# PEER expert layers: all tiles of the first table plain, a later use of 16 tokens' activations, eight tiles of the second table loaded early

## The chip, the cores and the metric

The kernel runs on one core of a Trainium2 chip. The core has TensorE (matmul; PE, with its weight loads PEld), VectorE (DVE), ScalarE (ACT), GpSimd (POOL) and SyncE (SP, which here issues DMAs), all working side by side on their own queues in program order, and 16 DMA engines. The metric is the device time of one execution in microseconds (us). The median of 3 runs of the kernel before is 1668.15 us (1666.73 to 1670.56).

## What is computed

A decoder trunk of two layers over 256 positions with 1024 features. Layer 0 is multi-head latent attention, layer 1 is native sparse attention; behind each stands a PEER feed-forward layer, and every sub-layer ends in a LayerNorm of `alpha * x + f(x)`. The change lies in the PEER layers, which run twice:

```python
def chunk(xc):
    q = (xc @ w_q).reshape(PEER_CHUNK, PEER_HEADS, 2, PEER_DK // 2)
    sc = jnp.einsum("thpd,hpnd->thpn", q, subkeys)
    s_half, i_half = lax.top_k(sc, PEER_TOPK)
    ...
    best, pos = lax.top_k(cand, PEER_TOPK)
    experts = jnp.take_along_axis(cand_idx, pos, axis=-1)
    g = jax.nn.softmax(best, axis=-1)
    u_e = u[experts]
    v_e = v[experts]
    a = jax.nn.gelu(jnp.einsum("thkd,td->thk", u_e, xc), approximate=False)
    return jnp.einsum("thk,thkd->td", (g * a), v_e)
```

So each token picks 8 x 16 = 128 of 16,384 experts, takes the gelu of its dot product with each picked row of table u, weighs it with the softmax `g`, and sums the picked rows of table v with these weights.

## The kernel before, in words

**Stages.** A PEER layer goes through three stages: projections and routing (`p_wq`, scores, top-k), then **u** (128 tiles of table u, each 128 experts x 1024 features), then **v** (128 tiles of table v). For 192 of the 256 tokens the kernel computes every expert: a u tile gives the dot products of 128 experts with these tokens on TensorE, their gelu goes into a store `A`, and the weight of an expert that a token did not pick is zero. Each of the last 64 tokens (`GT`) has its picked rows gathered from both tables by POOL instead; VectorE takes the dot products (`g_dot`, L554) in u and the weighted sums (`g_mac`, L582) in v. Of the 192 tokens, 176 (`NU`) get their u activations from the u tiles; the other 16 (`GX`) get theirs from gathered rows too, sent through a small DRAM buffer (`xdot` to `xD` to `xact`) and turned on TensorE in `x_weights` (L564).

**Plain and split tiles.** A tile of u is used in one of two ways, which `natural(j)` (L48) decides by the tile's number j. A *plain* tile (`nat`) is loaded straight into one of five places and multiplied in f32 with `xF`, the 176 tokens. A *split* tile goes through the weights' ring: it is loaded into one of four places of `raw4` (`raw`), ScalarE rounds it to `hi` (L157), VectorE takes the rest `lo` (L171), and TensorE multiplies `hi` with both halves of the activations side by side (352 columns) and `lo` with the high half (176 columns); ScalarE copies the second 176 columns out (`half`, L867) and VectorE adds them (L868). Tiles 0 to 43 and 122 to 127 are plain, of 44 to 111 three in four, of 112 to 121 one in three: 104 plain and 24 split ones per layer. The tiles of v are all split, and are loaded two at a time.

**Weights of the experts.** VectorE builds one-hots (`hot`, L731 and L736, for the last four groups L742) for four tokens at a time in `g_gen`. TensorE multiplies them in `g_flush` (`acc<-hot`), two groups at a time, at the beginning of a u tile when two are ready; VectorE and ScalarE put the product into `A` (L765, L767). The gelu of a tile comes one tile later in `u_fin` (L856), and its product with the weights (L859) a tile after that.

**What sets the order.** The program is written out in order by hand; each engine works down its own queue. Per u tile: the flush, the tile's matmuls, `u_fin` of the tile before, a portion of the one-hots by a budget (`run_side`), and about three row dot products in four tiles. `self.defer(n, f)` runs `f` n tiles later. Loads go out on SP in program order: `_snat` issues a plain tile five tiles ahead (`LEADN`), `_sdma` the ring's tiles as far as `_ahead` allows, never beyond `vlim`. `more_raw` opens four further places (`spare`), which lie where the activations `hT` lay; before, it is called at tile 121 of u. `end` closes each u tile and issues what `held` allows.

Of the kernel before, what the change touches and what calls it, by code (L numbers as in the profile page):

```python
# [24 lines left out]
P = 128  # L25
# [14 lines left out]
NROW = 6  # L40
RING, LEAD = 6, 1
LEADN = 5
LATE, LASTS = 112, 122
GB = 0.8
GS = 2.0 ** 15


def natural(j):  # L48
    return j < FIRST or j >= LASTS or (j % 4 != 3 if j < LATE else j % 3 == 0)


class Kern:
# [5 lines left out]
    def plan(self):  # L58
        I, L = self.I, []
        self.v0s, self.spare, self.pairs = [], None, {}  # L60
        self.nh, self.odd, self.nat, self.natural = 0, {}, set(), {}
        if "mla" in self.parts:
            L += [I["a_w_in"][k] for k in range(KC)]
            L += [I["a_wk"][i] for i in range(2)]
            L += [I["a_wq"][i] for i in range(3)]
            L += [I["a_wv"][i] for i in range(2)]
            L += [I["a_wq"][i] for i in range(3, 6)]
            L += [I["a_wo"][i] for i in range(KC)]
        for l in (0, 1):
            if l == 1 and "nsa" in self.parts:  # L70
                L += [I["s_wv"][i] for i in range(4)]
                L += [I["s_wT"][i] for i in range(4)]
                L += [I["b_wg"]]
                L += [I["s_wT"][i] for i in range(4, 8)]
                L += [I["b_wq"][i] for i in range(4)]
                L += [I["b_wq"][i] for i in range(4, 8)]
                L += [I["b_wo"][i] for i in range(KC)] + [I["b_wo"][i] for i in range(KC // 2)]
            if f"peer{l}" in self.parts:
                L += [I["p_wq"][l, i] for i in range(16)]
                self.nat.update(len(L) + j for j in range(P) if natural(j))  # L80
                self.odd.update((len(L) + j, 0) for j in range(P))
                L += [I["p_u"][l, (P - FIRST + j) % P] for j in range(P)]
                self.v0s.append(len(L))
                o = (len(L) - len(self.nat) - self.v0s[0] + sum(i < self.v0s[0] for i in self.nat)) % 4
                self.odd.update((len(L) + j, 1) for j in range(P))
                self.pairs.update((len(L) + j, I["p_v"][l, j:j + 2].rearrange("j i d -> i j d")) for j in range(o % 2, P - 1, 2))
                L += [I["p_v"][l, j] for j in range(P)]
        self.stream = L
        self.v0 = self.vb = self.v0s[0]
        self.rank = [0]  # L90
        for i in range(len(L) + 1):
            self.rank.append(self.rank[-1] + (i not in self.nat))
        self.si = 0
        self.used = 0
        self.sd = 0
        self.sn = 0
        self.slow, self.held, self.vlim = False, 0, 1 << 20
        self.sh = 0
        self.sl = 0
        self.raws, self.his, self.los = {}, {}, {}  # L100
        self.share = False
        self.alt = {}
        self.later, self.now = [], 0
# [101 lines left out]
    def end(self):  # L205

        self.used = self.si - 1
        self._snat()
        self.vlim += 2
        self._sdma(self.held)  # L210
        self.held = self._ahead()

# [286 lines left out]
    def peer(self, l):  # L499
        tc, nc, I = self.tc, self.nc, self.I  # L500
        self.v0 = self.v0s.pop(0)
        with ExitStack() as es:
            pool = lambda st, name: st.enter_context(tc.tile_pool(name=name, bufs=1, reuse_waits="tile"))

# [46 lines left out]
            def g_dot(k):  # L551
                a, c = order[k]
                t, x, d = grow.pop((a, c)), *((gacc, gdot) if a == "n" else (xrow, xdot))
                nc.vector.scalar_tensor_tensor(t, t, 1.0, x, op0=OP.mult, op1=OP.mult, accum_out=d[:, c:c + 1])  # L554
                if (a, c) == ("x", GX - 1):
                    g_row()
                    nc.scalar.activation(xdot, xdot, AF.Gelu)
                    self.defer(1, lambda: nc.gpsimd.dma_start(xD[1].rearrange("s t c -> (s t) c"), xdot))
                    self.defer(3, lambda: nc.gpsimd.dma_start(xact.rearrange("t (s c) -> t s c", s=P // GX),
                                                              xD[1].rearrange("s t c -> t s c")))  # L560
                    self.defer(6, x_weights)
                g_row()

            def x_weights():  # L564
# [268 lines left out]
            pu = None  # L833

            def u_step(j):
                hi, lo = self.nxt()
                ps = self.ps()
                if lo is None:
                    for k in range(KC):
                        self.mm(ps[:, 0:NU], hi[:, k * P:(k + 1) * P], xF[:, k, :], k == 0, k == KC - 1)  # L840
                else:

                    def high(k):
                        self.mm(ps[:, 0:2 * NU], hi[:, k * P:(k + 1) * P], self.hTT[:, k, :, 0:NU], k == 0, k == KC - 1)

                    for k in range(KC - 1):
                        high(k)
                    for k in range(KC):
                        self.mm(ps[:, 0:NU], lo[:, k * P:(k + 1) * P], xhi[:, k, 0:NU], False, False)
                    high(KC - 1)  # L850
                self.end()
                return j, ps, lo is not None

            due = deque()

            def u_fin(x):  # L856
                while due:
                    y, ps = due.popleft()
                    nc.vector.tensor_tensor(y, y, ps, op=OP.mult)  # L859
                if x is None:  # L860
                    return
                j, ps, wide = x
                jj = (P - FIRST + j) % P
                y, n = slot(jj), min(done["g"], NU)
                if wide:
                    t = gat.tile([P, NU], F32, tag="half", name="half", bufs=2)
                    nc.scalar.copy(t, ps[:, NU:2 * NU])  # L867
                    nc.vector.tensor_tensor(ps[:, 0:NU], ps[:, 0:NU], t, op=OP.add)  # L868
                if n:
                    nc.scalar.activation(ps[:, 0:n], ps[:, 0:n], AF.Gelu)  # L870
                    due.append((y[:, 0:n], ps[:, 0:n]))
                if n < NU:
                    nc.scalar.activation(y[:, n:NU], ps[:, n:NU], AF.Gelu)  # L873
                done["a"] = j + 1
# [22 lines left out]
                w_lo(1)  # L897

            dc, dj = 0, None
            self.slow, self.held = True, 0  # L900
            for j in range(P):
                if j == 5:
                    g_x()
                g_flush(2)
                x = u_step(j)
                if j == LASTS - 1:
                    self.slow, self.vlim = False, self.v0 + 1
                    self.more_raw()
                u_fin(pu)
                pu = x  # L910
                run_side(GB if len(A) > 1 else 2.2 if dj is None or j < dj else 1.4)
# [877 lines left out]
```

## Time and profile before

| What | Value |
|---|---|
| median of 3 runs | 1668.15 us |
| the profiled execution | 1670.8 us |
| its span, first to last instruction | 1669.0 us |
| mean granted TensorE clock | 0.993 |
| u of layer 0 and of layer 1, on TensorE | 168.65 to 513.46 us, 1024.86 to 1366.26 us |
| v of layer 0, on TensorE | from 513.46 to about 803 us |
| loads of u tiles | 208 plain, 48 split, 512 KB each |
| loads of v tiles | 127 pairs of 1024 KB, 2 single |
| HBM over the span | 295 GB/s |

The profile is one execution on the chip. A busy share is an average over stages with different limits, so the stages are read by windows. Matmuls are pipelined and their ends are modelled: the time of one is read from the start of one to the start of the next. In a row of a timeline stand the start, the time from the first start to the last end, engine, line, operation, tiles (out<-in) and count, and in brackets how long the engine was idle before it and what released it. A plain f32 matmul of the program stands as two instructions in the profile, so a plain tile has 16.

### The profile page before, as it was taken

The page shows a single profiled execution, that of the slowest core. Times are in us where ns is not written, and L with a number is a line of the kernel's source. Part 1 is how long each engine was busy: PE and PEld are TensorE (multiplying, and loading weights), DVE is VectorE, ACT ScalarE, POOL GpSimd, SP SyncE. Part 2 cuts the span into 40 slices and gives each one's busy share as a digit, 9 for nine tenths or more (in the row PEclk, how much of TensorE's full clock was granted, in tenths as well). Part 3 has the DMA queues.
Part 4 walks back from the last instruction along what each step waited for, and adds up shares of the span by engine and source line. Part 5 has one row for each costly group of instructions (what it writes and reads, how often), then busy time and mean ns, then how long its engine had stood idle before and what let it go on. Part 6 is the DMA issues. An engine that isn't in the chain of part 4 may idle for free.

```text
span 1669.0 us, 28191 instructions
## 1 busy us (share of the span) xinstructions
PE 1605.8 (96%) x9988; PEld 1441.3 (86%) x9988; DVE 1438.9 (86%) x3437; ACT 777.4 (47%) x1675; POOL 524.6 (31%) x426
## 2 busy tenths in 40 slices
PE   7999999999989999999997999999999999999997
PEld 6879999899988888888885789999999898888886
DVE  6788698799987999999778789688899969999998
ACT  6655212333345555556466853123333345555554
POOL 2011133333334444441342211334333325444430
PEclk9999999999999999999999999999999999999999
DMA  7528899899978999998583258999999889999992
GB/s 243 189 84 262 295 362 368 307 342 341 335 274 337 387 359 349 356 356 311 172 257 95 70 193 270 315 410 326 348 338 338 300 305 385 359 354 350 364 347 90
DMA packets 136301, 494.10 MB, mean 296 GB/s; under 512 B 13888, under 2 KB 17120, under 8 KB 135072
## 3 DMA queue, kind: packets, MB, share of 16 engines
q1 hardware_dynamic: 90416, 325.75, 55.5%
q0 software_dynamic: 45744, 166.55, 26.7%
q8 instruction: 79, 1.29, 0.3%
q14 instruction: 62, 0.51, 0.1%
HBM read 486.44 MB, written 5.28 MB: 295 GB/s over the span
## 4 chain that ended last, share of the span: by engine, by line
PE 71%; DVE 18%; issue 4%; DMA 3%; ACT 3%; POOL 1%; SPq 0%; DVEq 0%; ACTq 0%; POOLq 0%
PE acc L252 42%; PE mm L252 28%; DVE row L554 5%; DVE lo L171 2%; PE mm L279 1%; DVE idx L612 1%; DMA nat<-p_u 1%; DVE hot L731 1%; DVE hot L736 1%; ACT hi L157 1%; POOL row L541 1%; DVE vals L610 1%; DVE A L765 1%; DMA raw<-a_wv 1%; DMA xact<-xD 1%
## 5 line engine op out<-in xcount | busy, mean ns | idle before, releaser
L252 PE MATMUL mm<-xF,nat 128*128 128x176 f32 x3328 | 511.9, 314 | 0.0
L252 PEld LDWEIGHTS mm<-xF,nat 128*128 128x128 f32 x3328 | 499.7, 190 | 0.1
L252 PE MATMUL acc<-hi,W 128*128 128x512 f32 x1452 | 410.6, 391 | 0.0
L541 POOL DMA_INDIRECT row<-p_v,gidx x128 | 244.9, 1913 | 333.1 <-DVE gacc L582 247.1
L171 DVE TENSOR_TENSOR lo<-raw,hi 128x1024 fp32r<-128x1024 f32 (+1 forms) x251 | 307.6, 1231 | 34.9 <-ACT hi L157 28.6
L157 ACT CAST hi<-raw 128x1024 fp32r<-128x1024 f32 (+1 forms) x255 | 265.4, 1045 | 141.1 <-PE acc L252 115.5
L252 PEld LDWEIGHTS acc<-hi,W 128*128 128x128 f32 x1452 | 272.5, 188 | 59.2
L252 PE MATMUL acc<-lo,W 128*128 128x512 f32 x968 | 299.7, 391 | 0.0
L541 POOL DMA_INDIRECT row<-p_ur,gidx x128 | 150.2, 1173 | 303.6 <-DVE row L554 160.8
L252 PEld LDWEIGHTS acc<-lo,W 128*128 128x128 f32 x968 | 181.7, 188 | 39.6
L157 ACT CAST hi<-spare 128x1024 fp32r<-128x1024 f32 x122 | 128.4, 1053 | 112.3 <-PE acc L252 110.3
L252 PE MATMUL mm<-hT,hi 128*128 128x256 f32 (+1 forms) x1040 | 168.6, 305 | 0.0
L582 DVE SCALAR_TENSOR_TENSOR gacc<-row,ggate,gacc 128x1024 f32<-128x1024 f32 x126 | 161.4, 1281 | 0.0
L171 DVE TENSOR_TENSOR lo<-spare,hi 128x1024 fp32r<-128x1024 f32 x122 | 149.2, 1223 | 13.1 <-ACT hi L157 12.9
L554 DVE SCALAR_TENSOR_TENSOR row<-row,gacc 128x1024 f32<-128x1024 f32 x128 | 156.5, 1223 | 0.0
L252 PEld LDWEIGHTS mm<-hT,hi 128*128 128x128 f32 x1040 | 143.6, 190 | 1.9 <-issue 1.2
L873 ACT ACTIVATE A<-mm 128x176 f32<-128x176 f32 (+21 forms) x220 | 60.2, 274 | 169.1 <-PE mm L252 144.1
L767 ACT ACTIVATE A<-acc 128x176 f32<-128x176 f32 (+15 forms) x132 | 37.1, 313 | 160.6 <-DVE A L765 132.9
L889 DVE TENSOR_TENSOR W<-A,W 128x128 fp32r<-128x128 f32 (+1 forms) x512 | 108.0, 254 | 3.2 <-ACT W L884 3.2
L870 ACT ACTIVATE mm<-mm 128x176 f32<-128x176 f32 (+21 forms) x170 | 42.4, 249 | 122.2 <-PE mm L252 86.6
L252 PE MATMUL mm<-hT,lo 128*128 128x176 f32 (+1 forms) x712 | 94.4, 275 | 0.0
L252 PEld LDWEIGHTS mm<-hT,lo 128*128 128x128 f32 x712 | 90.6, 192 | 0.0
(292 smaller groups left out, 1864.5 us busy)
## 6 DMA issues: line engine op xcount, KB each, us to landing
nat<-p_u SPq DMA_DIRECT2D x208, 512.0 KB
spare<-p_v SPq DMA_DIRECT2D x64, 1024.0 KB
raw<-p_v SPq DMA_DIRECT2D x63, 1024.0 KB
raw<-p_u SPq DMA_DIRECT2D x48, 512.0 KB
raw<-p_wq SPq DMA_DIRECT2D x32, 512.0 KB
raw<-b_wo SPq DMA_DIRECT2D x12, 512.0 KB
raw<-a_wo SPq DMA_DIRECT2D x8, 512.0 KB
raw<-s_wT SPq DMA_DIRECT2D x8, 512.0 KB
```

The lines of the kernel that those rows point to most:

```text
L157: self.nc.scalar.copy(self.his[i], self.raws[i])
L171: e.tensor_tensor(self.los[i], raw, self.his[i].bitcast(F32), op=OP.subtract)
L252: self.nc.tensor.matmul(out, a, b, start=start, stop=stop)
L279: self.nc.tensor.transpose(out, in_, self.ident[:n, :n])
L541: nc.gpsimd.indirect_dma_start(out=t, out_offset=None, in_=table, in_offset=bass.IndirectOffsetOnAxis(ap=at, axis=0))
L554: nc.vector.scalar_tensor_tensor(t, t, 1.0, x, op0=OP.mult, op1=OP.mult, accum_out=d[:, c:c + 1])
L582: nc.vector.scalar_tensor_tensor(gacc, t, ggate[:, c:c + 1], gacc, op0=OP.mult, op1=OP.add)
L610: nc.vector.max(out=v[:, c], in_=s); yield 0.24
L767: nc.scalar.activation(x[:, m:n, t0:t0 + 4], pv[:, j0 + m:j0 + n], AF.Copy, scale=sc_)
L870: nc.scalar.activation(ps[:, 0:n], ps[:, 0:n], AF.Gelu)
L873: nc.scalar.activation(y[:, n:NU], ps[:, n:NU], AF.Gelu)
L889: nc.vector.tensor_tensor(WW[j][:, o:o + c.stop - c.start], slot(j)[:, c], WW[j][:, c].bitcast(F32), op=OP.subtract)
```

## The change

Three things change, in both PEER layers.

- All 128 tiles of u are plain: `natural` is gone, and with it the split branch of `u_step`, the `half` copy and its sum in `u_fin`.
- `x_weights` is deferred by 20 tiles in place of 6.
- `more_raw` is called before the first tile of u in place of tile 121, as no tile of u reads `hT` any more. `vlim` stops the ring ahead of v until u begins, then opens two tiles of v, and two more every fourth tile. So the first eight tiles of v (in layer 1 a single one and three pairs) are loaded in the first part of u into the four `raw` places and the four `spare` places.

```diff
-LATE, LASTS = 112, 122
+LASTS = 122
...
-def natural(j):
-    return j < FIRST or j >= LASTS or (j % 4 != 3 if j < LATE else j % 3 == 0)
...
-                self.nat.update(len(L) + j for j in range(P) if natural(j))
+                self.nat.update(len(L) + j for j in range(P))
...
         self.used = self.si - 1
         self._snat()
-        self.vlim += 2
         self._sdma(self.held)
         self.held = self._ahead()
...
         self.v0 = self.v0s.pop(0)
+        self.vlim = self.v0 - 1
...
-                    self.defer(6, x_weights)
+                    self.defer(20, x_weights)
...
             def u_step(j):
-                hi, lo = self.nxt()
+                w, _ = self.nxt()
                 ps = self.ps()
-                if lo is None:
-                    for k in range(KC):
-                        self.mm(ps[:, 0:NU], hi[:, k * P:(k + 1) * P], xF[:, k, :], k == 0, k == KC - 1)
-                else:
-
-                    def high(k):
-                        self.mm(ps[:, 0:2 * NU], hi[:, k * P:(k + 1) * P], self.hTT[:, k, :, 0:NU], k == 0, k == KC - 1)
-
-                    for k in range(KC - 1):
-                        high(k)
-                    for k in range(KC):
-                        self.mm(ps[:, 0:NU], lo[:, k * P:(k + 1) * P], xhi[:, k, 0:NU], False, False)
-                    high(KC - 1)
+                for k in range(KC):
+                    self.mm(ps[:, 0:NU], w[:, k * P:(k + 1) * P], xF[:, k, :], k == 0, k == KC - 1)
                 self.end()
-                return j, ps, lo is not None
+                return j, ps
...
-                if wide:
-                    t = gat.tile([P, NU], F32, tag="half", name="half", bufs=2)
-                    nc.scalar.copy(t, ps[:, NU:2 * NU])
-                    nc.vector.tensor_tensor(ps[:, 0:NU], ps[:, 0:NU], t, op=OP.add)
...
-            self.slow, self.held = True, 0
+            self.slow, self.held, self.vlim = True, 0, self.v0 + 1
+            self.more_raw()
             for j in range(P):
...
                 x = u_step(j)
+                if j % 4 == 1:
+                    self.vlim += 2
                 if j == LASTS - 1:
-                    self.slow, self.vlim = False, self.v0 + 1
-                    self.more_raw()
+                    self.slow = False
```

Three places show how the instructions stand. SP's queue around the beginning of u in layer 0, before (`raw<-p_u` are split tiles, `nat<-p_u` plain ones):

```order
L128 DMA raw<-p_wq 128x1024
L591 DMA subT<-p_sub 128x256
L128 DMA raw<-p_u 128x1024 x2
L139 DMA nat<-p_u 128x1024
L128 DMA raw<-p_u 128x1024
L139 DMA nat<-p_u 128x1024
L128 DMA raw<-p_u 128x1024
L139 DMA nat<-p_u 128x1024 x48
L128 DMA raw<-p_u 128x1024
L139 DMA nat<-p_u 128x1024 x3
```

and of the change:

```order
L124 DMA raw<-p_wq 128x1024
L587 DMA subT<-p_sub 128x256
L135 DMA nat<-p_u 128x1024 x4
L119 DMA raw<-p_v 128x2x1024
L135 DMA nat<-p_u 128x1024 x5
L119 DMA raw<-p_v 128x2x1024
L135 DMA nat<-p_u 128x1024 x4
L119 DMA spare<-p_v 128x2x1024
L135 DMA nat<-p_u 128x1024 x4
L119 DMA spare<-p_v 128x2x1024
L135 DMA nat<-p_u 128x1024 x111
```

The split tiles' loads are gone, and four pairs of v stand among the first 17 plain tiles; then 111 plain tiles follow with nothing between them.

TensorE's queue of layer 0 where the 16 tokens' activations are turned (`ident,xact`), before; it is the first instruction behind a flush:

```order
L252 MATMUL acc<-hot 128x128
L279 MATMUL mm<-ident,xact 128x16
L252 MATMUL mm<-xF,nat 128x176 x8
L252 MATMUL mm<-hT,hi 128x352 x7
L252 MATMUL mm<-hT,lo 128x176 x8
L252 MATMUL mm<-hT,hi 128x352
L252 MATMUL mm<-xF,nat 128x176 x8
L252 LDWEIGHTS hot
```

and of the change, some 130 rows further down the queue:

```order
L247 MATMUL acc<-hot 128x128
L247 MATMUL mm<-xF,nat 128x176 x8
L274 MATMUL mm<-ident,xact 128x16
L247 MATMUL mm<-xF,nat 128x176 x16
L247 LDWEIGHTS hot
```

The transpose has moved behind 14 further tiles, and the split tile's 16 matmuls (`hT,hi` and `hT,lo`) have become 8 of a plain tile.

VectorE's queue of layer 0 between two flushes about 60 us later, before:

```order
L765 SCALAR_TENSOR_TENSOR A_2860<-acc,A_2860 128x21x4
L859 TENSOR_TENSOR A_2860<-A_2860,mm 128x80
L868 TENSOR_TENSOR mm<-mm,half 128x176
L731 TENSOR_TENSOR hot<-iota_87,selI 128x1024
L736 TENSOR_TENSOR hot<-hot,selG 128x1024
L554 SCALAR_TENSOR_TENSOR row,gdot<-row,gacc 128x1024
L171 TENSOR_TENSOR lo<-raw,hi 128x1024
L859 TENSOR_TENSOR A_2860<-A_2860,mm 128x88
L731 TENSOR_TENSOR hot<-iota_87,selI 128x1024
L554 SCALAR_TENSOR_TENSOR row,gdot<-row,gacc 128x1024
L859 TENSOR_TENSOR A_2860<-A_2860,mm 128x88
L736 TENSOR_TENSOR hot<-hot,selG 128x1024
```

and of the change, at the same place:

```order
L761 SCALAR_TENSOR_TENSOR A_2861<-acc,A_2861 128x21x4
L844 TENSOR_TENSOR A_2861<-A_2861,mm 128x80
L727 TENSOR_TENSOR hot<-iota_87,selI 128x1024
L732 TENSOR_TENSOR hot<-hot,selG 128x1024
L550 SCALAR_TENSOR_TENSOR row,gdot<-row,gacc 128x1024
L844 TENSOR_TENSOR A_2861<-A_2861,mm 128x88
L727 TENSOR_TENSOR hot<-iota_87,selI 128x1024
L550 SCALAR_TENSOR_TENSOR row,gdot<-row,gacc 128x1024
L844 TENSOR_TENSOR A_2861<-A_2861,mm 128x88
L732 TENSOR_TENSOR hot<-hot,selG 128x1024
```

`lo` and the sum with `half` are gone; the other instructions stand in the same order. The same holds elsewhere in u, and POOL's queue is the same as before.

More of the change, by code (lines that the diff above doesn't have):

```diff
@@ L861, in u_fin @@
                     return
-                j, ps, wide = x
+                j, ps = x
                 jj = (P - FIRST + j) % P
                 y, n = slot(jj), min(done["g"], NU)
-                if wide:
-                    t = gat.tile([P, NU], F32, tag="half", name="half", bufs=2)
-                    nc.scalar.copy(t, ps[:, NU:2 * NU])
-                    nc.vector.tensor_tensor(ps[:, 0:NU], ps[:, 0:NU], t, op=OP.add)
                 if n:
```

## The prediction

> **What bounds the kernel now.** I read the page's busy shares first, then the windows of the u stage (168.65 to 513.46 us in layer 0, 1024.86 to 1366.26 us in layer 1) and of the v stage behind it, then who waited for whom on TensorE, then the timelines of TensorE and VectorE around the longest waits. A row of the windows view holds busy us and instructions of PE, PEld, DVE, ACT and POOL, then the granted clock, the DMA share and GB/s.
>
> ```profile
> PE 1605.8 (96%) x9988; PEld 1441.3 (86%) x9988; DVE 1438.9 (86%) x3437; ACT 777.4 (47%) x1675; POOL 524.6 (31%) x426
> ...
> 168.00:216.00 48.00, 47.93 (x324) 47.90 (x324) 33.24 (x176) 10.99 (x26) 6.98 (x8) 1.00 0.87 288
> 224.00:272.00 48.00, 48.00 (x325) 47.99 (x324) 41.78 (x145) 9.24 (x23) 16.38 (x15) 1.00 1.03 409
> 280.00:300.00 20.00, 16.02 (x117) 15.75 (x116) 15.18 (x42) 5.20 (x20) 8.13 (x9) 0.91 0.83 318
> 300.00:340.00 40.00, 39.99 (x317) 39.59 (x316) 34.34 (x84) 14.88 (x48) 13.03 (x12) 1.00 0.89 315
> 300.00:460.00 160.00, 155.35 (x1228) 153.61 (x1227) 144.10 (x352) 55.95 (x185) 52.69 (x45) 1.00 0.93 333
> 460.00:490.00 30.00, 25.61 (x201) 24.59 (x200) 29.62 (x61) 12.74 (x36) 9.38 (x7) 0.94 0.74 255
> 514.00:660.00 146.00, 146.00 (x645) 120.88 (x645) 139.38 (x232) 84.86 (x131) 68.45 (x35) 1.00 0.95 354
> 1320.00:1340.00 20.00, 18.49 (x142) 17.65 (x142) 19.64 (x44) 9.12 (x25) 5.46 (x4) 0.91 0.86 297
> ```
>
> TensorE is the bound. In v it has no gap at all (146.00 of 146.00), so data that is there earlier can gain nothing in v. In u it is idle only in places, and three windows have a lower clock besides. The waits of TensorE, first for 168 to 514 us, then for 1024 to 1367 us (total, times, longest):
>
> ```profile
> PE acc L252 <- DVE hot L736: 8.0, 7, 2.8
> PE mm L279 <- DMA xact<-xD: 4.0, 1, 4.0
> PE acc L252 <- DVE hot L742: 1.4, 4, 0.6
> ...
> PE acc L252 <- DVE hot L736: 8.0, 7, 2.7
> PE mm L279 <- DMA xact<-xD: 2.2, 1, 2.2
> PE acc L252 <- DVE hot L742: 1.4, 4, 0.6
> ```
>
> These 25.0 us are nearly all that can be won. No plain tile (`nat`) is among the releasers.
>
> **Plain against split.** The timeline of TensorE:
>
> ```profile
> 316.30 4.99 PE L252 MATMUL mm<-xF,nat 128*128 128x176 f32 x32
> 321.00 1.40 PE L252 MATMUL mm<-hT,hi 128*128 128x352 f32 x7
> 322.24 1.03 PE L252 MATMUL mm<-hT,lo 128*128 128x176 f32 x8
> 323.11 0.35 PE L252 MATMUL mm<-hT,hi 128*128 128x352 f32 x1
> 323.30 1.09 PE L252 MATMUL acc<-hot 128*128 128x128 f16 x16
> 324.23 7.38 PE L252 MATMUL mm<-xF,nat 128*128 128x176 f32 x48
> 331.44 1.25 PE L252 MATMUL acc<-hot 128*128 128x128 f16 x16
> ```
>
> Durations overlap, so I take start to start. A plain tile is 16 instructions: two tiles take 321.00 - 316.30 = 4.70 us, three take 331.44 - 324.23 = 7.21 us, so 2.35 to 2.40 us each. A split tile takes 323.30 - 321.00 = 2.30 us. Thus plain tiles save TensorE nothing: 48 tiles cost 0.05 to 0.10 us more each, **+3.9 us** at 0.08.
>
> **The waits for one-hots.** What they cost is on VectorE. The first flush of layer 0 on TensorE; then VectorE's timeline between two later flushes, and TensorE's row at the end of it:
>
> ```profile
> 275.57 0.62 PE L252 MATMUL acc<-hot 128*128 128x128 f16 x8 [0.62 <-DVE hot L736]
> ...
> 367.11 1.11 DVE L765 SCALAR_TENSOR_TENSOR A<-acc,A 128x176 f32<-128x176 f32 x6 [0.47 <-PE acc L252]
> ...
> 369.83 0.35 DVE L868 TENSOR_TENSOR mm<-mm,half 128x176 f32<-128x176 f32 x1 [1.47 <-ACT half L867]
> ...
> 372.56 1.22 DVE L171 TENSOR_TENSOR lo<-raw,hi 128x1024 fp32r<-128x1024 f32 x1
> ...
> 375.75 0.69 DVE L736 TENSOR_TENSOR hot<-hot,selG 128x1024 f16<-128x1024 f16 x1
> ...
> 376.50 0.62 PE L252 MATMUL acc<-hot 128*128 128x128 f16 x8 [1.29 <-DVE hot L736]
> ```
>
> From 367.11 to the end of the last one-hot at 376.44 VectorE needs 9.3 us, while TensorE has three plain tiles (7.2 us) before it asks. The change takes out `lo` (1.22), `half` (0.35) and the wait for `half` (1.47): 3.0 us, which leaves 6.3 us, under the 7.2. So the wait of 1.29 us goes, with 0.9 us in hand, and the same holds for the others between tiles 44 and 121. The stretch as a whole says the same (line groups of TensorE and VectorE, 300 to 460 us: count, busy us, mean ns, idle before):
>
> ```profile
> L252 PE MATMUL mm<-xF,nat 128*128 128x176 f32 x700 | 109.8, 314 | 0.0
> ...
> L554 DVE SCALAR_TENSOR_TENSOR row<-row,gacc 128x1024 f32<-128x1024 f32 x44 | 53.8, 1222 | 0.0
> ...
> L171 DVE TENSOR_TENSOR lo<-raw,hi 128x1024 fp32r<-128x1024 f32 x14 | 17.1, 1220 | 0.0
> ...
> L868 DVE TENSOR_TENSOR mm<-mm,half 128x176 f32<-128x176 f32 x15 | 5.2, 350 | 10.2 <-ACT half L867 9.9
> ```
>
> VectorE's 144.1 us lose 22.3, so 122 us stand beside about 156 us of TensorE. The 2 x 8.0 us hold one wait of 0.6 per layer (at 275.57) that comes before the first split tile and stays; of the other 14.8 I take **-13.5**, since a stretch with three rows between flushes can still come out short (bounds 0 and -14.8). The `L742` waits stand among the densest split tiles: **-2.0** of 2.8 (bounds 0 and -2.8).
>
> **The 16 tokens' activations.** Chain of waits, then TensorE:
>
> ```profile
> 282.80 8.17 DMA xD<-xdot
> ...
> 291.56 4.52 DMA xact<-xD
> ...
> 296.21 0.20 PE L279 MATMUL mm<-ident,xact 16*128 16x16 f32 x1 [3.98 <-DMA xact<-xD]
> 296.35 3.88 PE L252 MATMUL mm<-xF,nat 128*128 128x176 f32 x13
> ...
> 467.14 0.97 PE L252 MATMUL acc<-hot 128*128 128x128 f16 x8 [2.75 <-DVE hot L736]
> ```
>
> The round trip ends 13.3 us after its start (282.80 to 296.08); 20 tiles give it about 48 us, and the weights are needed only by the last four groups, past 467 us. The transpose moves behind 14 further tiles and waits for nothing: **-6.2 us** (4.0 + 2.2).
>
> **The clock.** Behind the waits of 3.98 and 2.75 us TensorE runs slower: the eight flush matmuls at 467.14 show 0.97 us where they show 0.62 at 376.50. The three windows with 0.91, 0.94 and 0.91 lose 20 x 0.09 + 30 x 0.06 + 20 x 0.09 = 5.4 us. With no long wait they stay at 1.00: **-5.4 us**.
>
> The Trainium skill, "TensorE: Matmul & The Clock Gate", Part 1, lets the clock halve only after an idle window of some 3.4 us. The trace agrees for 3.98 us, not for 2.75 us, which halved it in both layers; if those two had another cause, the sum would be 3.6 us smaller.
>
> **The eight early tiles.** They go out on SP between plain tiles, one pair per four or five tiles, by about tile 17. Their 4.2 MB (8 x 0.524) fall into 168 to 216 us, where DMA moves 288 GB/s against 409 in the next stretch: room for (409 - 288) x 48 us = 5.8 MB. Their places are free: the raw ones since the last `p_wq` tile was split, `spare` since the last projection read `hT`, both before tile 0 of u ends. What SP waits for before it issues a plain tile (168 to 514 us), and SP's timeline at the end of u:
>
> ```profile
> SPq L139 <- PE mm L252: 247.3, 89, 8.4
> ...
> 497.79 0.38 SPq L123 DMA_DIRECT2D raw<-p_v  x1
> 499.26 2.90 SPq L139 DMA_DIRECT2D nat<-p_u  x2
> ```
>
> A plain tile (512 KB) goes out when TensorE releases the one five back and has four tiles, 9.5 us, to land. From 224 to 272 us all tiles are plain, DMA is full, and TensorE does not wait, so 9.5 us suffice; nor does it wait for the two plain tiles that follow a pair at 497.79. Cost **0**, gain in v **0** (bounds: +20 us, below, and 0).
>
> **The sum**, against the profiled execution (1670.8 us; span 1669.0): -13.5 - 2.0 - 6.2 - 5.4 + 3.9 = -23.2, so 1647.6. The median of the runs shown is 1668.15, 2.65 lower, so 1645.
>
> **Rivals.**
> - *VectorE stays late.* Only the activations' wait and its clock loss go: -6.2 - 1.8 + 3.9 = -4.1, 1664. With half of the one-hot waits and their clock loss back it is -23.2 + 7.75 + 3.6 = -11.9, 1656. For it: VectorE was also held by rows and flushes. Against it: the 3.0 us counted above. 10%.
> - *The early tiles hold up the plain ones.* A pair (1.05 MB) takes 2.6 us at 409 GB/s. If nothing hid the eight pairs' worth of it, TensorE would lose 8 x 2.6 = 21 us: 1666. Against it: 9.5 us of lead. The Trainium skill, "DMA: Bandwidth & Descriptors", "Queues, rings and completion order", says that each DMA engine takes a ring's descriptors in order, so a plain tile has the whole pair ahead of it; the two tiles behind the pair at 497.79 came in time all the same. 4%.
> - *Slower: DMA becomes the bound from tile 44 on.* Split tiles had places of their own and were fetched further ahead; now all 84 tiles come through five. The stretch 300 to 460 us moved 333 x 160 = 53.3 MB for 58.75 tiles (700 / 16 plain and 15 split), 0.907 MB a tile. TensorE's 155.4 busy us with 15 x 0.08 more are 156.6, so 2.66 us a tile, and that asks for 341 GB/s. If the mix delivered only 315, the lowest window above, a tile took 2.88 us: 168 x 0.22 = +37, with -23 a net +14, 1682. It decides below 0.907 / (2.66 + 23.2 / 168) = 324 GB/s. Against it: 409 GB/s where asked for. 8%, in 5 of which it ends slower.
> - *The change does not do what it says:* excluded, since the order above has the moves.
>
> **How the numbers follow.** Forecast 78%: 1639 (all 25.0 and 5.4 go, plain tiles at +0.05: -28.0, and a restart of 0.05 to 0.1 us saved at some 20 waits) to 1652.7 (half of the one-hot waits stay, 7.75, with the clock at 1.00). The range reaches into the first rival: 1639 to 1657. About 0.2% (3.3 us) is what a measurement of this kernel can tell from no change: faster 0.89, within it 0.05, slower 0.06, the last from the DMA rival and a little of the second.
>
> **What would show it.** Right: no `xact` wait on TensorE; `hot` waits below 2 us per layer; granted clock 1.00 in all of u; 128 plain tiles at 2.35 to 2.40 us; u about 11.6 us shorter per layer, v unchanged. Wrong: `nat` as releaser of TensorE, in the first 17 tiles for the early loads, after tile 44 for DMA; or `hot` waits with VectorE still over 90% busy from tile 44 on.

## The result, and the profile after

| | before | after |
|---|---|---|
| median of the comparison | 1669.36 us (4 runs) | 1655.86 us (4 runs) |
| ratio | | 0.9921 (95% interval 0.9902 to 0.9940) |
| profiled execution | 1670.8 us | 1655.8 us |
| its span | 1669.0 us | 1653.7 us |
| u of layer 0 | 344.81 us | 335.32 us |
| u of layer 1 | 341.40 us | 335.40 us |

The change makes the kernel 13.5 us faster. The forecast was 1645 us, a gain of 23; the result lies inside the range of 1639 to 1657, close to its upper end. The length of u is read on TensorE, from the start of the first plain tile to the start of the first matmul of v. In the changed kernel those are the rows 169.04 and 504.36 us in layer 0, 1015.77 and 1351.17 us in layer 1. The line numbers of the program move with the change: matmuls are now L247, one-hots L727 and L732 (those of the last four groups L738), row dot products L550, single loads L124, pairs L119, plain tiles L135.

TensorE's waits in the changed kernel, first for 160 to 514 us (layer 0), then for 1000 to 1360 us (layer 1), in total, times, longest:

```profile
PE mm L247 <- DVE sc L611: 1.9, 1, 1.9
PE acc L247 <- DVE hot L732: 0.6, 1, 0.6
...
PE mm L247 <- DMA nat<-p_u: 3.4, 1, 3.4
PE acc L247 <- DVE hot L732: 0.6, 1, 0.6
```

Of the 25.0 us of waits that the forecast was after, only the 0.6 per layer is left that it had set aside. Two new ones stand there, and both are for a matmul of a plain tile. The window rows that answer to those of before (busy us and instructions of PE, PEld, DVE, ACT and POOL, then granted clock, DMA share, GB/s):

```profile
168.00:216.00 48.00, 45.99 (x298) 45.55 (x298) 33.20 (x174) 10.66 (x24) 6.54 (x8) 0.96 0.91 335
...
280.00:300.00 20.00, 20.00 (x159) 19.90 (x158) 15.94 (x40) 6.79 (x31) 8.79 (x9) 1.00 0.94 339
...
300.00:460.00 160.00, 160.00 (x1244) 158.85 (x1243) 130.19 (x338) 38.21 (x156) 56.23 (x47) 1.00 0.96 348
460.00:490.00 30.00, 30.00 (x241) 29.84 (x240) 19.52 (x49) 6.49 (x26) 8.29 (x8) 1.00 0.98 352
...
514.00:660.00 146.00, 146.00 (x645) 120.91 (x644) 139.20 (x231) 84.08 (x130) 68.26 (x37) 1.00 0.97 363
1320.00:1340.00 20.00, 20.00 (x151) 19.95 (x150) 7.35 (x18) 4.03 (x16) 3.83 (x3) 1.00 0.93 332
```

From 280 us on TensorE has no gap and the clock is 1.00, as forecast. VectorE has 130.2 busy us in 300 to 460 us where it had 144.1, and it now waits for TensorE at a flush instead of the other way round (VectorE's timeline of the changed kernel, at the same flushes):

```profile
366.49 1.10 DVE L761 SCALAR_TENSOR_TENSOR A<-acc,A 128x176 f32<-128x176 f32 x6 [1.80 <-PE acc L247]
...
374.62 1.13 DVE L761 SCALAR_TENSOR_TENSOR A<-acc,A 128x176 f32<-128x176 f32 x6 [0.60 <-PE acc L247]
...
382.76 1.16 DVE L761 SCALAR_TENSOR_TENSOR A<-acc,A 128x176 f32<-128x176 f32 x6 [1.62 <-PE acc L247]
```

So VectorE has 0.6 to 1.8 us in hand per flush; the forecast had worked out 0.9 for one. (It had 122 us for the stretch; as tiles pass faster, the stretch also holds more rows and one-hots than before.) What is lost lies in the first 50 us of u, where 168 to 216 us shows 45.99 busy us and a clock of 0.96.

**The new waits.** The chain of what ended last, at the beginning of u in layer 1 of the changed kernel (start us, us, what):

```profile
1034.88 12.10 PE mm L247 x81
1046.98 0.02 issue
1046.99 13.48 DMA nat<-p_u
1060.47 0.14 issue
1060.61 14.41 PE mm L247 x95
```

and SP's timeline there:

```profile
1044.98 0.43 SPq L119 DMA_DIRECT2D spare<-p_v  x1
1046.99 33.31 SPq L135 DMA_DIRECT2D nat<-p_u  x13
```

The plain tile issued at 1046.99, directly behind an early pair of v, took 13.48 us to land. TensorE was ready for it at 1060.61 - 3.38 = 1057.23, 10.2 us after the issue. In layer 0 the view of waits puts the wait down to VectorE's `sc` (L611), a step of the top-k that no matmul of a plain tile reads. The timelines of SP and TensorE in layer 0 say otherwise:

```profile
198.25 0.43 SPq L119 DMA_DIRECT2D spare<-p_v  x1
200.26 2.71 SPq L135 DMA_DIRECT2D nat<-p_u  x2
...
212.05 61.61 PE L247 MATMUL mm<-xF,nat 128*128 128x176 f32 x400 [1.94 <-DVE sc L611]
```

The transfers of the same kernel issued between 200 and 201.5 us (what, queue, count, KB, us to landing):

```profile
nat<-p_u SPq DMA_DIRECT2D x1, 512.0 KB, 11.7
```

The tile issued at 200.26 landed 11.7 us later, at 211.96, and TensorE goes on at 212.05. It too is a plain tile behind an early pair; VectorE's instruction only ended at the same moment. For comparison, plain tiles issued from 168 to 186 us, with an early pair among them but before any row is gathered, and from 224 to 272 us, beside rows but with no pair (count, KB, median us to landing):

```profile
nat<-p_u SPq DMA_DIRECT2D x8, 512.0 KB, 4.9
...
nat<-p_u SPq DMA_DIRECT2D x20, 512.0 KB, 8.1
```

Why just there? POOL issues its first five row gathers (0.5 MB each) between 190.4 and 196.5 us. The windows of 8 us in before, and in the changed kernel:

```profile
200.00:208.00 8.00, 8.00 (x56) 7.99 (x56) 5.38 (x36) 1.15 (x4) 0.00 (x0) 1.00 1.03 409
208.00:216.00 8.00, 8.00 (x56) 8.00 (x55) 7.96 (x55) 0.95 (x3) 0.97 (x1) 1.00 0.81 257
```

```profile
200.00:208.00 8.00, 8.00 (x56) 7.99 (x55) 4.98 (x33) 1.19 (x4) 0.00 (x0) 1.00 1.02 412
208.00:216.00 8.00, 6.06 (x30) 5.82 (x29) 7.97 (x54) 0.39 (x2) 0.58 (x1) 0.79 0.96 374
```

Before the change DMA was already full from 200 to 208 us (409 GB/s); the 288 GB/s that the forecast read for 168 to 216 us was a mean over 48 us. The last row also shows a clock of 0.79 behind a wait of 1.94 us, which costs 8 x 0.21 = 1.7 us. The DMA queues of the changed kernel from 201.5 to 206 us (q0 holds POOL's gathers, q1 SP's loads; packets, MB, share of the 16 engines):

```profile
q0 software_dynamic: 262, 0.95, 51.9%
q1 hardware_dynamic: 258, 0.93, 51.2%
```

With gathers in flight they take half of DMA, and SP's loads move 0.93 MB in 4.5 us. At that rate, as an estimate, a plain tile alone (0.52 MB) takes 2.5 us, and one with a pair ahead of it (1.57 MB together) 7.6 us.

### The profile page after: what moved, and what is told of

The parts are those of the page before. It is cut to its first block, busy times and chain, and to the rows that moved or that the text cites. A ratio compares the mean times of both kernels' runs of the same rounds, so it can differ in the third digit from the quotient of the medians.

```text
span 1653.7 us, 28004 instructions
## 1 busy us (share of the span) xinstructions
PE 1609.5 (97%) x9988; PEld 1448.2 (88%) x9988; DVE 1371.8 (83%) x3341; ACT 718.4 (43%) x1579; POOL 508.7 (31%) x426
## 4 chain that ended last, share of the span: by engine, by line
PE 90%; DVE 5%; ACT 2%; DMA 2%; issue 1%; SPq 0%; POOL 0%; ACTq 0%
PE mm L247 46%; PE acc L247 43%; PE mm L274 1%; DMA nat<-p_u 1%; DMA xT<-xT 0%; DMA bounce<-ropeO 0%; DVE lo L167 0%; DVE bnst L321 0%; ACT hi L153 0%; DVE row L550 0%; ACT p L1653 0%; DVE m L1646 0%; ACT p L1650 0%; DVE hN L343 0%; DVE idx L608 0%
## 5 line engine op out<-in xcount | busy, mean ns | idle before, releaser
L247 PE MATMUL mm<-xF,nat 128*128 128x176 f32 x4096 | 625.4, 314 | 5.3 <-DMA nat<-p_u 3.4
L247 PEld LDWEIGHTS mm<-xF,nat 128*128 128x128 f32 x4096 | 612.8, 191 | 6.3 <-issue 6.2
L247 PE MATMUL acc<-hi,W 128*128 128x512 f32 x1452 | 410.9, 391 | 0.0
L537 POOL DMA_INDIRECT row<-p_v,gidx x128 | 231.3, 1807 | 343.7 <-DVE gacc L578 256.4
L247 PEld LDWEIGHTS acc<-hi,W 128*128 128x128 f32 x1452 | 272.7, 188 | 58.9
L247 PE MATMUL acc<-lo,W 128*128 128x512 f32 x968 | 300.1, 391 | 0.0
L153 ACT CAST hi<-raw 128x1024 fp32r<-128x1024 f32 (+1 forms) x207 | 215.2, 1045 | 142.5 <-PE acc L247 115.8
L167 DVE TENSOR_TENSOR lo<-raw,hi 128x1024 fp32r<-128x1024 f32 (+1 forms) x203 | 247.8, 1227 | 34.7 <-ACT hi L153 29.6
L247 PEld LDWEIGHTS acc<-lo,W 128*128 128x128 f32 x968 | 181.8, 188 | 39.4
L550 DVE SCALAR_TENSOR_TENSOR row<-row,gacc 128x1024 f32<-128x1024 f32 x128 | 155.8, 1217 | 0.0
L761 DVE SCALAR_TENSOR_TENSOR A<-acc,A 128x176 f32<-128x176 f32 (+19 forms) x244 | 48.7, 265 | 65.1 <-PE acc L247 64.7
L865 ACT CAST W<-A 128x192 fp32r<-128x192 f32 x256 | 88.3, 347 | 0.0
L247 PE MATMUL mm<-hT,hi 128*128 128x256 f32 x656 | 85.1, 282 | 0.0
L247 PEld LDWEIGHTS mm<-hT,hi 128*128 128x128 f32 x656 | 79.0, 188 | 1.9 <-issue 1.2
```

The lines of the kernel that those rows point to most:

```text
L153: self.nc.scalar.copy(self.his[i], self.raws[i])
L167: e.tensor_tensor(self.los[i], raw, self.his[i].bitcast(F32), op=OP.subtract)
L247: self.nc.tensor.matmul(out, a, b, start=start, stop=stop)
L537: nc.gpsimd.indirect_dma_start(out=t, out_offset=None, in_=table, in_offset=bass.IndirectOffsetOnAxis(ap=at, axis=0))
L761: nc.vector.scalar_tensor_tensor(y, pv[:, j0:j0 + m], 1.0 / GS, y, op0=OP.mult, op1=OP.mult)
L865: nc.scalar.copy(WW[j][:, 0:ND], slot(j))
```

## The experiments

The theory after the result: what the forecast took from split tiles and the activations came, and the early tiles of v cost what is missing, because a pair ahead of a plain tile in SP's order delays that tile. Rivals: the loss belongs to TensorE or VectorE (plain tiles cost more than thought), or it is the burst of five gathers alone, or chance. Each time is a median; the ratio is against the kernel before on the same chip, which had 1671.04 us (13 runs) beside `e1` to `e4`, 1670.88 us (9 runs) beside `e5` to `e8` and 1671.53 us (9 runs) beside `r1`, `r2` and `e9`. "u" gives the lengths in layers 0 and 1.

**No early loads** (`e1_no_early`): the changed kernel, with v opened at tile 121 as before.

```diff
-            self.slow, self.held, self.vlim = True, 0, self.v0 + 1
-            self.more_raw()
+            self.slow, self.held = True, 0
...
+                if j >= LASTS:
+                    self.vlim += 2
...
-                if j % 4 == 1:
-                    self.vlim += 2
                 if j == LASTS - 1:
-                    self.slow = False
+                    self.slow, self.vlim = False, self.v0 + 1
+                    self.more_raw()
```

> The changed kernel without the early loads: the first tiles of v are loaded from tile 121 of u on. Theory (the early loads, together with the burst of gathered rows, made plain tiles late around tile 17): TensorE's wait of 1.9 us with its halved clock (1.7) in layer 0 and of 3.4 us in layer 1 are gone, 7.0 us less than the changed kernel, about 1649. Rival (the burst of rows alone does it): the waits stay, about 1656. In both, v's first tiles now come late: a wait at the start of v of up to 5 us per layer would say what the early loads are good for.

Measured: 1648.76 us (1647.94 to 1651.33), ratio 0.9867 [0.9850, 0.9884]; u 331.43 and 331.43 us. TensorE's waits, layer 0 (those of layer 1 are the same row):

```profile
PE acc L247 <- DVE hot L732: 0.6, 1, 0.6
```

Both new waits are gone, and with them 335.32 + 335.40 - 2 x 331.43 = 7.9 us of u. v does not begin later, and from the end of u in layer 0 to the beginning of u in layer 1 it takes 511.6 us, against 511.4 with early loads. So the early loads cost 7.9 us and bring nothing; without them the gain is 22.3 us, where 23.2 was forecast for the sum.

**The two again on one chip** (`r1_after_again`, the changed kernel; `r2_no_early_again`, the kernel without early loads).

> The changed kernel as it is, beside the kernel without the early loads on the same chip. Theory (the early pairs of v hold up one plain tile per layer, and that costs the u stages some 8 us together): about 1656, with one wait for a plain tile of 1.5 to 3.5 us in the first 20 tiles of u in each layer, and a median 6 to 9 us above that of the kernel without early loads. Rival (the difference of the first two comparisons came from the stage between the two u stages, whose length varies): the medians are within 3 us.

> The changed kernel without the eight early tiles of v, the same as tried before, beside the changed kernel. Theory: about 1648.5, u of both layers about 331.4 us, TensorE's only wait in u 0.6 us per layer. Rival (the gain was chance): above 1652.

Measured: 1656.62 us (1655.53 to 1658.70), ratio 0.9905 [0.9888, 0.9921], and 1650.48 us (1648.13 to 1651.42), ratio 0.9869 [0.9851, 0.9886]. The difference is 6.1 us, and u is 335.17 and 336.03 against 331.44 and 331.43 us. TensorE's waits for plain tiles in the changed kernel are 1.3 and 1.8 us in layer 0 (two places, not one) and 2.2 us in layer 1. The view of waits names VectorE for the last two; the tiles that TensorE goes on with are again those directly behind a pair, and they land 10.7, 13.2 and 12.4 us after their issue. The loss is no chance; its size changes from run to run.

**Early pairs ahead of the rows** (`e6_pairs_0_8`): the changed kernel, with the four pairs out by tile 9, before POOL's first gather.

```diff
-                if j % 4 == 1:
+                if j in (0, 2, 4) or j % 4 == 1 and j > 8:
                     self.vlim += 2
```

> The changed kernel with its four pairs issued by tile 9 in place of tile 17, so that they go out ahead of the five gathered rows. Theory (a pair and rows must be in flight together): no wait for nat, or one below 1 us, about 1649. Rival (pairs so close behind each other add up to 440 GB/s with the plain tiles, more than the 409 seen): waits for nat within the first ten tiles, 1652 or above.

Measured: 1650.10 us (1648.55 to 1652.18), ratio 0.9873 [0.9856, 0.9890]; u 331.93 and 331.99 us, no wait for a plain tile. SP's timeline:

```profile
165.09 0.39 SPq L119 DMA_DIRECT2D raw<-p_v  x1
...
176.70 0.43 SPq L119 DMA_DIRECT2D raw<-p_v  x1
...
181.47 0.43 SPq L119 DMA_DIRECT2D spare<-p_v  x1
...
186.24 0.43 SPq L119 DMA_DIRECT2D spare<-p_v  x1
188.25 20.05 SPq L135 DMA_DIRECT2D nat<-p_u  x9
```

The same four pairs, packed closer, but all issued before the gathers begin (190.4 us in the changed kernel), cost 0.5 to 0.6 us per layer. A pair alone does not delay a plain tile enough; a pair and gathered rows together do.

**Early pairs among ordinary rows** (`e4_early_from_90`): opened from tile 90 on, far from the burst.

```diff
-            self.slow, self.held, self.vlim = True, 0, self.v0 + 1
-            self.more_raw()
+            self.slow, self.held = True, 0
...
-                if j % 4 == 1:
+                if j == 89:
+                    self.vlim = self.v0 + 1
+                    self.more_raw()
+                if j > 89 and j % 4 == 1:
                     self.vlim += 2
```

> The changed kernel with the same eight early loads, moved from tiles 0 to 17 to tiles 90 to 110. Theory (only the meeting with the burst of five rows makes plain tiles late): no wait for nat, 7 us less than the changed kernel, about 1649. Rival (a pair in front of plain tiles holds them up anywhere while rows are gathered): waits for nat between tiles 93 and 112, 1652 or above.

Measured: 1656.51 us (1654.91 to 1665.07), ratio 0.9904 [0.9888, 0.9920]; u 335.07 and 338.65 us. (The profiled execution took 1665.07 us, the longest of the five, and part of that has nothing to do with u: from the end of one u to the beginning of the next it takes 516.9 us, against 511.4 in the changed kernel.) SP's timeline, TensorE's, and the transfers' counts for 425 to 460 us (count, KB):

```profile
417.77 0.43 SPq L119 DMA_DIRECT2D raw<-p_v  x1
419.78 8.46 SPq L135 DMA_DIRECT2D nat<-p_u  x4
428.29 0.43 SPq L119 DMA_DIRECT2D spare<-p_v  x1
430.30 8.46 SPq L135 DMA_DIRECT2D nat<-p_u  x4
438.81 0.43 SPq L119 DMA_DIRECT2D spare<-p_v  x1
...
445.10 7.47 PE L247 MATMUL mm<-xF,nat 128*128 128x176 f32 x48 [3.40 <-DMA nat<-p_u]
...
DMA packets 3828, 14.02 MB, mean 401 GB/s; under 512 B 411, under 2 KB 411, under 8 KB 3826
...
row<-p_ur,gidx POOLq DMA_INDIRECT x10
```

A pair goes out every 428.29 - 417.77 = 10.52 us, with four plain tiles and, at 10 gathers in 35 us, three rows: 9 x 0.524 = 4.7 MB, which asks for 448 GB/s where 401 are delivered. The plain tile directly behind the third pair, issued at 430.30, lands after 14.67 us; TensorE, ready for it after 11.4 us, waits 3.4 us, in layer 1 3.8 us. So the rival was right here: the burst of five gathers is not needed, ordinary rows do it.

**Single tiles for pairs** (`e5_singles`): the eight early tiles as eight loads of 512 KB, one per two tiles of u.

```diff
-                self.pairs.update((len(L) + j, I["p_v"][l, j:j + 2].rearrange("j i d -> i j d")) for j in range(o % 2, P - 1, 2))
+                self.pairs.update((len(L) + j, I["p_v"][l, j:j + 2].rearrange("j i d -> i j d")) for j in range(8 + o % 2, P - 1, 2))
...
-            self.slow, self.held, self.vlim = True, 0, self.v0 + 1
+            self.slow, self.held, self.vlim = True, 0, self.v0
...
-                if j % 4 == 1:
-                    self.vlim += 2
+                if j % 2 == 1:
+                    self.vlim += 1
```

> The changed kernel with the early tiles of v loaded one at a time, one for every two tiles of u, in place of one pair for every four: the same bytes over the same tiles. Theory (a plain tile queues behind the 1 MB pair in front of it, and the 1.4 us that a landing of 8.1 us leaves of the 9.5 us do not cover it; half a pair fits nearly): TensorE's waits for nat fall below 2 us per layer, about 1650. Rival (too many bytes in this stretch, whatever their grain): waits as in the changed kernel, about 1656.

Measured: 1651.93 us (1651.16 to 1655.72), ratio 0.9888 [0.9869, 0.9906]; u 334.05 and 332.36 us, waits for plain tiles 2.1 and 0.3 us. The same bytes in halves cost 2.6 + 0.9 = 3.5 us of u in place of 7.9. So the size of what stands ahead of a plain tile counts, and the amount as well, since 3.5 us are still lost. No run puts the pairs on another queue, which would part the two.

**The activations' deferral alone** (`e2_split_20`, the kernel before with 20 for 6) **and its undoing** (`e3_plain_6`, the kernel without early loads with 6 for 20).

```diff
-                    self.defer(6, x_weights)
+                    self.defer(20, x_weights)
```

> The kernel before with the 20 tiles' deferral alone. Theory (the terms add up): the wait for xact (4.0 + 2.2) and one halved clock (1.8) go, all one-hot waits stay at 8.0 per layer: 8 us less than the kernel before, about 1661. Rival (VectorE caught up during the xact wait): one-hot waits grow above 8.0 per layer and take back half or more, 1664 or above.

> The kernel without early loads, all tiles plain, but with the 6 tiles' deferral. Theory (the parts are independent): one-hot waits 0.6 per layer as in the changed kernel, the xact wait of about 4.0 and 2.2 us and a halved clock are back: 8 us more than the kernel without early loads and with 20. Rival (the xact wait too came from VectorE being late): it shrinks below 2 us per layer, and the two kernels differ by less than 4 us.

Measured for the first: 1666.81 us (1664.30 to 1667.11), ratio 0.9969 [0.9958, 0.9980]: 4.2 us gained where 8 were expected, so the rival's time and not the theory's. u is 339.72 and 339.42 us, 5.1 and 2.0 less than before. The waits for `xact` are gone, in layer 0 also the slow clock behind it, but waits for one-hots grew (layer 1 here, layer 0 the same with 8.6 and 1.4):

```profile
PE acc L252 <- DVE hot L736: 8.6, 7, 2.7
PE acc L252 <- DVE hot L742: 2.7, 4, 1.9
```

In layer 1 they take back 0.6 + 1.3 of the 2.2 us. What u gains there is another thing: the window 1320 to 1340 us, at 0.91 before, is at 1.00, although the wait for one-hots ahead of it is still there (2.74 us, 2.75 before). Nothing in this edit explains that.

Measured for the second: 1657.43 us (1655.99 to 1661.81), ratio 0.9920 [0.9905, 0.9935]; u 335.88 and 333.41 us, 4.45 and 1.98 more than without it. The waits for `xact` are back with 2.8 and 2.0 us, and one slow stretch (the window 290 to 310 us at 0.91, 20 x 0.09 = 1.8 us): 2.8 + 1.8 and 2.0, as found. Beside plain tiles the step is worth 6.4 us of u. Beside split ones it gives 5.1 us in layer 0 and, without the stretch at 1320 us (1.8 us), next to nothing in layer 1, because what it frees there is waited for at the flushes.

**What made VectorE late** (`e7_lo_load`, the size of `lo` added back to VectorE at the 24 tiles that were split; `e8_half_wait`, the `half` copy and a sum added back there). Both are the kernel without early loads, and the results of the added instructions are not used.

```diff
+                if 44 <= j < LASTS and (j % 4 == 3 if j < 112 else j % 3 != 0):
+                    nc.vector.tensor_tensor(self.raw4[:, 0], self.raw4[:, 1], self.raw4[:, 2], op=OP.subtract)
```

```diff
+                if 44 <= j < LASTS and (j % 4 == 3 if j < 112 else j % 3 != 0):
+                    t = gat.tile([P, NU], F32, tag="half", name="half", bufs=2)
+                    nc.scalar.copy(t, ps[:, 0:NU])
+                    nc.vector.tensor_tensor(ps[:, 256:256 + NU], ps[:, 0:NU], t, op=OP.add)
```

> The kernel without early loads, all tiles plain, with one VectorE instruction of lo's size (128 x 1024, 1.22 us) put back at each of the 24 tiles that were split; its result is not used. Theory (VectorE's load as such made the one-hots late, lo being the larger part): one-hot waits of 2 to 5 us per layer come back, 1653 to 1659. Rival (VectorE was late because it stood waiting for half): one-hot waits stay at 0.6 per layer, about 1649.

> The kernel without early loads, all tiles plain, with ScalarE's copy half and VectorE's sum with it put back at the 24 tiles (0.35 us and the wait for ScalarE); the sum goes to unused columns. Theory (lo's load is the larger part): one-hot waits below 2 us per layer, 1649 to 1652. Rival (the wait for half is what made VectorE late): 3 us or more per layer, 1655 or above. If both this and the run with lo's load show few waits, only the two together overfill the time between flushes.

Measured: 1654.70 us (1653.82 to 1655.52), ratio 0.9900 [0.9881, 0.9919], u 333.74 and 333.70 us, and 1650.58 us (1649.50 to 1652.17), ratio 0.9874 [0.9855, 0.9893], u 331.44 and 331.42 us. TensorE's waits in layer 0 of the first:

```profile
PE acc L247 <- DVE hot L738: 1.3, 2, 1.1
PE acc L247 <- DVE hot L732: 0.6, 1, 0.6
```

Neither alone brings the 8.0 us back. `lo` alone fits between the flushes and is late only at the last four groups, where one flush takes 3.3 us in place of 1.4 and the next 1.7 (those are nearly the 2.3 us of u); the sum with `half` and the wait for it alone (4.9 and 10.5 us in all from 300 to 460 us) fit everywhere. With 0.6 to 1.8 us in hand per flush it takes both, 3.0 us, to overfill them; the kernel before shows them together, no run adds both to plain tiles.

**Split tiles in the first 44** (`e9_split_first`): the kernel without early loads, with 11 of tiles 0 to 43 split in each layer; the first flush of one-hots comes behind them.

```diff
-                self.nat.update(len(L) + j for j in range(P))
+                self.nat.update(len(L) + j for j in range(P) if j >= FIRST or j % 4 != 3)
```

(with the split branch of `u_step` and the `half` sum of before).

> The kernel without early loads, with every fourth one of tiles 0 to 43 split again (11 per layer; tiles 44 to 127 stay plain). Theory (a plain tile costs TensorE about 0.12 us more than a split one, and in the first 44 tiles VectorE has no lo or half to spare but some 6 of 48 us free): where nothing waits, u is 11 x 0.12 = 1.3 us shorter per layer, 330.1 each, so about 1646. Rival (VectorE's 11 lo of 1.22 us and 11 sums of 0.35 us overfill it in the part where one-hots and rows are densest): waits for one-hots of 0.5 to 1 us at each flush in tiles 4 to 43, u 333 or more, so 1651 to 1655.

Measured: 1656.86 us (1654.52 to 1660.59), ratio 0.9903 [0.9886, 0.9921]; u 336.25 and 336.26 us. Two of TensorE's waits in layer 0 (a third, for ScalarE, is 0.2 us) and the window row of 224 to 272 us:

```profile
PE acc L247 <- DVE hot L732: 2.1, 2, 1.7
PE mm L247 <- DVE lo L167: 2.1, 3, 1.2
...
224.00:272.00 48.00, 45.91 (x308) 44.35 (x306) 47.52 (x163) 13.64 (x31) 18.95 (x15) 1.00 0.95 346
```

The rival was right that VectorE is overfilled: 41.78 of 48 us busy there before, it is at 47.52. But TensorE waits for `lo` and at one flush, where the rival had every flush late. Without the waits (4.4 us) and the clock of 0.92 from 280 to 300 us (1.6 us), u would be 330.2 us, 0.6 less than the 330.8 of the kernel without early loads; 11 x 0.12 = 1.3 had been expected. Split tiles do cost TensorE a little less, but neither these first tiles nor those from 44 on have the VectorE time for them.

## Why the prediction was right or wrong

Terms in us, both layers together. Clock terms are from the window rows, 1 - clock times their length. The row of the plain tiles is what u grew by, net, beside the waits and clock terms.

| Step of the prediction | forecast | measured |
|---|---|---|
| waits for one-hots, L736 | -13.5 | -14.8 (16.0 to 1.2) |
| waits L742 | -2.0 | -2.8 |
| wait for `xact` | -6.2 | -6.2 |
| clock | -5.4 | -5.4, and +1.7 behind a new wait |
| 48 plain tiles for split ones | +3.9 | +5.8 |
| eight early tiles | 0 | +5.3 of waits (1.9 + 3.4) |
| sum | -23.2 | -16.4 |

The lengths of u say 335.32 + 335.40 - 344.81 - 341.40 = -15.5, so 0.9 us of the sum stay unassigned.

- **What bounds it, right.** TensorE; nothing was to be gained in v: 146.00 of 146.00 before and after.
- **One-hots, right in mechanism and nearly in size.** The forecast removed `lo`, `half` and the wait for `half`, 3.0 us, and found the rest to fit. The two kernels that add one of them back show that each alone is borne between most flushes and that the waits came from both together. The 1.3 us kept back for "a stretch with three rows" were not needed.
- **Activations, right beside plain tiles.** Moved back there they cost 6.4 us of u, the waits and one slow stretch. Moved alone, beside split tiles, they gave 7.1 us of u, of which 1.8 have no cause in the edit and 1.9 of layer 1's 2.2 came back as waits for one-hots: the step needs the first one.
- **The clock, right where the waits went.** All three windows are at 1.00, the two behind a 2.75 us wait among them; that one of these was also gone with the deferral alone, its wait unchanged, shows that part of this term can come and go. The rule in the Trainium skill, "TensorE: Matmul & The Clock Gate", Part 1, that an idle window of some 3.4 us is needed, does not hold for single waits here: 1.94 us slowed the clock in the changed kernel, 3.38 us did not. The forecast did right to take the row.
- **Plain tiles, mis-sized.** The forecast read +0.08 us per tile from the starts of tiles. A whole round from flush to flush says more, and two stand in the prediction's own rows: three plain tiles take 331.44 - 324.23 = 7.21 us, two plain ones and a split one 323.30 - 316.30 = 7.00. That is 0.21 per tile, 24 x 0.21 = 5.0 us per layer. (The plain tile ahead of the split one looked short because the two overlap: 316.30 + 4.99 = 321.29, but the split one starts at 321.00.) u grew by less. Without early loads it is 331.43 - 0.6 = 330.8 us free of waits in both layers. Before, free of waits and of the slow clock, it was 344.81 - 13.4 - 3.6 = 327.8 us in layer 0 and 341.40 - 11.6 - 1.8 = 328.0 us in layer 1: +2.9 per layer. The two fit if each of the 11 waits that went had cost some 0.2 us more than its idle time. One such wait is left, in the first flush of the changed kernel:

```profile
278.60 0.62 PE L247 MATMUL acc<-hot 128*128 128x128 f16 x8
279.85 0.62 PE L247 MATMUL acc<-hot 128*128 128x128 f16 x8 [0.62 <-DVE hot L732]
280.31 7.37 PE L247 MATMUL mm<-xF,nat 128*128 128x176 f32 x48
```

Cut in two by a wait of 0.62 us, this flush takes 280.31 - 278.60 = 1.71 us; an uncut one takes 324.23 - 323.30 = 0.93. So the wait costs 0.16 us more than it shows. The prediction put this restart at 0.05 to 0.1 us, without a row for it, and only in its range. That every wait costs as much is not shown. The split tiles tried among the first 44 give 0.6 / 11 = 0.05, with stops that may hide a part in the same way.
- **The eight early tiles, wrong: this step failed.** The prediction put their cost at 0, as there was "room for (409 - 288) x 48 us = 5.8 MB" and "9.5 us suffice". The room was a mean: in 8 of these 48 us DMA was full. And neither piece of evidence had a pair and rows at once: from 224 to 272 us there are rows and no pair, and after the pair at 497.79 us no gather is issued until u ends (before's last one goes out at 493.74, and gathers have 20.0% of DMA from 486 to 512 us). The runs showed what stands in its place: a plain tile lands in 4.9 us (168 to 186 us, no rows), in 8.1 us beside rows (224 to 272 us), and in 10.7 to 15.4 us beside rows directly behind a pair, against a lead of 10 to 11. The rival "the early tiles hold up the plain ones" had 4% and 21 us; it is what happened, at 7.9 us, since only the last one or two of the four pairs meet the rows and the lead takes up part of each.
- **DMA as the bound from tile 44 on** did not come: 348 GB/s from 300 to 460 us and no wait, where the rival had 341 as the need. The run with early loads from tile 90 shows where it does: 448 GB/s were asked for and 401 came.

The Trainium skill, "DMA: Bandwidth & Descriptors", "Queues, rings and completion order", says that each DMA engine works a ring's descriptors off in order. A plain tile behind a pair on SP's queue then has the whole pair ahead of it. The runs agree: the tile directly behind the pair is the late one, and halving the pair's size cut the loss from 7.9 to 3.5 us. The prediction cited it and let one row with few gathers outweigh it.

That the time still came inside the range was luck as far as this step goes. The range ended at 1657 for another rival, one-hot waits that stay, which did not come; the rival that came stood at 1666, outside, and cost 7.9 us in place of 21. The version that beats both kernels is the one without early loads: 1648.76 and 1650.48 us in two comparisons, ratios 0.9867 and 0.9869.

## What to carry to other kernels

A load that is fetched early for nobody is not free because DMA has room on average: take the window in which it lies, add up what every queue asks for there, and compare the time that the most urgent tile then needs with its lead. Evidence that a transfer comes in time counts only from a stretch with the same company. When a step of several edits pays, try the kernel without each: here one of three gave a third of the others' gain back.

## What the runs showed of the hardware that was not expected

- The length of a single wait does not decide whether the clock slows. In the changed kernel 1.94 us did (the window 208 to 216 us at 0.79) and 3.38 us did not (1056 to 1064 us at 1.00); on its repeat 1.8 us did not and 2.2 us did; with early loads from tile 90, 3.40 us did not and 3.81 us did. At the same flush of layer 1, 2.75 us did in the kernel before and 2.74 us did not with the deferral alone. The Trainium skill, "TensorE: Matmul & The Clock Gate", Part 1, describes a free-running window; that it is the phase of the wait against this window that decides fits these rows, but no run here moves the phase alone.
- A wait can be put down to the wrong engine: the layer 0 wait is shown as VectorE's, and the landing of the tile (211.96 us) shows that it was DMA. It goes when the early loads go, with VectorE's work unchanged.
